# State updates of the running streams from operands already on chip: masked copies of B and 32-row products in place of two DRAM round trips

## The chip, the cores and the metric

The kernel runs on one core of one Trainium2 chip. The metric is device time in microseconds of one execution; the median of several is given. The engines are called by their short names in the profile: PE is the matrix engine (PEld its weight loads), DVE is VectorE, ACT is ScalarE, POOL is GpSimd, SP is the queue that issues most transfers. PSUM is the memory that PE writes its products to, in banks of 512 floats per partition; SBUF is the on-chip memory that everything else works in.

## The reference

One step of a layer with two parallel branches (causal pooling, and a Mamba-2 state-space branch, SSD) and an MLP, for 256 frames of a new stream and 16 frames each of 8 running streams, 384 rows in all. Model width 2048, 64 heads of 64 in 8 groups, state size 128, one layer, all in float32. The change concerns the last line of the scan, the new state of the running streams:

```python
def step(h, inp):
    xc, dtc, Bc, Cc = inp
    cum = jnp.cumsum(dtc * A, axis=1)
    ...
    xdt = xc * dtc[..., None]
    ...
    last = cum[:, -1]
    w_end = jnp.exp(last[:, None] - cum)
    h = h * jnp.exp(last)[..., None, None] + jnp.einsum('bsgn,bsgr,bsgrp->bgrpn', Bc, w_end, xdt)
    return h, y
```

For each of the 8 streams, group g and head, the new state is the decayed old one plus a sum over that stream's 16 frames of B (128 values a frame) times the weighted input (64 values a frame).

## The kernel before

Activations are held transposed (channels on partitions, 384 rows along the free axis). Every large product is done in three passes of a 32-bit matrix format: each operand is split into a high part h (a ScalarE copy that rounds) and a low part l (VectorE subtracts h from the original), and PE adds h·h, h·l and l·h. Weights come in slices of 128x1024 by an SP transfer (`wfetch`, line 63) and are split by lines 70 and 71 into three buffers each; `take` keeps up to three slices split ahead.

The state-space stage (lines 543 to 929) runs over eight groups g. In each, PE makes ten projections of two slices each: B, C, four blocks of x, four of the gate z (tiles `pj_x` and `pj_z`). The first six pass through a causal convolution (`conv_in`, `taps`, tiles cbuf, cacc, xs), which reads the old convolution state from `cstate`. Between projections stand short runs of small products, called lumps. A group has two pairs of channel blocks, jp = 0 and 1, and each pair S (four heads) has:

- `t_trx`: x is transposed to frames on partitions (`trx`, two PSUM banks); VectorE multiplies it by step-size weights into `xdt` and `xdw` (`xside`), and `xdw` is split into `xhl`, high and low (lines 729, 730);
- `t_trB`, once a group: B transposed the same way, split into `Bhl` (lines 685, 686);
- `t_cb` and `mside`: products of C and B, masked into `cbm`; `eside`: exponentials `E` on ScalarE;
- `t_yi`: the old states times C; `dside`: the old states `hs` are decayed; `t_Y`, `t_yT`: the outputs Y;
- `t_pp`: the new stream's state from `Bhl` and `xhl`;
- `state` (`t_su`, line 771 on): the running streams' update, eight products into four PSUM banks `su`, which VectorE adds to `hs` (line 786); then POOL's queue stores `hs`.

A lump is appended to PE's order with `lump`, so PE runs the lumps and projections in program order; on the other engines a scheduler orders the instructions at build time, by estimated times and by when tiles come free. Mid-group the order is pp, trx, cb, trB, yT, Y, yi and then su of the pair before; at the group's end it is pp, trx, yT, Y, yi, su.

In the block of the running streams, rows of `Bhl` and `xhl` are frames: stream b holds partitions 16b to 16b+15. A product that contracts over partitions can separate streams only if they lie on rows of their own, and PE's row strips begin at multiples of 32 or 64. The kernel before therefore stores the running streams' part of `Bhl` and `xhl` to DRAM (`b_scr`, `x_scr`, lines 688 and 733) and loads it back rearranged into `bst` and `xst` (lines 692 and 737): each stream gets 64 rows, four blocks of its 16 frames, with the four combinations of high and low parts of the two operands. One product over 64 rows then gives a stream's update with all its splits at once. Two streams stand on the two halves of the rows, and four positions along the free axis hold the eight streams.

All PSUM results outside the accumulating `mm` tiles (two banks) come from a pool of six banks, `sstile`. SBUF pools of a stage are stacked, so their tiles lie where tiles of the stage before were, and their first writes wait for those. `phd` holds most tiles of this stage and `phd1`, on top of it, the convolution state `cstate`, the buffers `cbuf` and, before the change, `bst`.

Of the kernel before, what the change touches and what calls it, by code (L numbers as in the profile page):

```python
# [6 lines left out]
F32 = mybir.dt.float32  # L7
F32R = mybir.dt.float32r
I32 = mybir.dt.int32
AF = mybir.ActivationFunctionType  # L10
ALU = mybir.AluOpType
# [3 lines left out]
P = 128  # L15
# [3 lines left out]
TS_ = 16  # L19
DM = 2048  # L20
KD = DM // P
G = 8
# [5 lines left out]

C_IDENT, C_ONES, C_MASK, C_CM, C_BM = 0, 128, 256, 768, 1024
C_RC, C_SCAN, C_END = 1032, 1096, 1504  # L30
V_GPRE, V_GMLP, V_PSC, V_CW, V_CB, V_NRM, V_DSK, V_DTB, V_ALOG, V_END = 0, 16, 32, 48, 240, 288, 320, 352, 353, 384


def build(ctx, tc, io):
    nc = tc.nc
    v, s, te, gp, sy = nc.vector, nc.scalar, nc.tensor, nc.gpsimd, nc.sync
# [5 lines left out]
    dram = ctx.enter_context(tc.tile_pool(name="dram", bufs=1, space=DRAM))  # L42
# [3 lines left out]
    vec = consts.tile([P, V_END], F32, name="vec")  # L46
# [6 lines left out]
    def sstile(name):  # L53
        return pss.tile([P, 512], F32, tag="ss", name=name)
# [27 lines left out]
    def woven(a):  # L82
        return a.rearrange("p (a n) -> p n a", a=2)

    def pairs(a):
        return a.rearrange("p (n a) -> p n a", a=2)
# [111 lines left out]
    a_scr = [dram.tile([P, T], F32, name=f"a_scr{i}") for i in range(32)]  # L198
    ma_scr = [dram.tile([P, T], F32, name=f"ma_scr{i}") for i in range(KD)]
    gb_scr = [dram.tile([P, T], F32, name=f"gb_scr{i}") for i in range(KD)]  # L200
    b_scr = [dram.tile([P, 2, P], F32, name=f"b_scr{i}") for i in range(G)]
    x_scr = [dram.tile([P, 2, 2, P], F32, name=f"x_scr{i}") for i in range(16)]
    cum_scr = dram.tile([NH, T], F32, name="cum_scr")
    dec_scr = dram.tile([NH, NB], F32, name="dec_scr")

# [149 lines left out]
    with tc.tile_pool(name="phc", bufs=1, reuse_waits="tile") as pc, tc.tile_pool(name="phc2", bufs=2, reuse_waits="tile") as pc2:  # L355
        pst = pc.tile([P, KD, NB, 15], F32, name="pst")
        gp.dma_start(pst, io["state_pool"])
        bufs = []
# [184 lines left out]
    with tc.tile_pool(name="phd", bufs=2, reuse_waits="tile") as pd, tc.tile_pool(  # L543
        name="phd1", bufs=1, reuse_waits="tile"
# [4 lines left out]
        for i in range(3):  # L549
            b = pd1.tile([P, 24, 19], F32, name=f"cbuf{i}")  # L550
            gp.memset(b[:, 0, :3], 0.0)
            cbuf.append(b)
        bst = []
        for i in range(2):
            bst.append(pd1.tile([P, 4, P], F32R, name=f"bst{i}"))
        seg = lambda a: a.rearrange("p (b t) -> p b t", b=24)
        ncv = [0]

# [33 lines left out]
        def lump(fn):  # L592
            with behind(last[0]):
                last[0] = fn()
# [87 lines left out]
        def bside(D):  # L682
            D.Bhl = pd.tile([P, 2, 3, P], F32R, tag="Bhl", name=f"Bhl{D.g}")
            bh, bl = (D.Bhl[:, a].rearrange("p b n -> p (b n)") for a in range(2))
            s.activation(bh, D.tr[:, :T], AF.Copy)
            v.tensor_tensor(bl, D.tr[:, :T], bh.bitcast(F32), ALU.subtract)
            bscr = b_scr[D.g]
            sy.dma_start(bscr, D.Bhl[:, :, 2, :].bitcast(F32))
            D.bs = bst[D.g % 2]
            for p4 in range(4):  # L690
                for h2 in range(2):
                    sy.dma_start(
                        D.bs[h2 * 64 + p4 * 16 : h2 * 64 + p4 * 16 + 16].bitcast(F32),
                        bscr.rearrange("(q h r) l n -> h l r q n", q=4, h=2)[h2, p4 // 2],
                    )

        def cside(D):
            D.Cm = pd.tile([P, 2, P], F32, tag="Cm", name=f"Cm{D.g}", bufs=1)
# [11 lines left out]
        def xside(S):  # L710
            S.xdt = pd.tile([P, 2, 3, P], F32, tag="xdt", name=f"xdt{S.nm}")
            S.xdw = pd.tile([P, 2, 3, P], F32, tag="xdw", name=f"xdw{S.nm}", bufs=1)
            for q, tv in enumerate(S.trs):
                for o, i in ((S.xdt, 3), (S.xdw, 6)):
                    v.tensor_tensor(
                        o[:, q].rearrange("p b (h q) -> p b h q", h=2),
                        tv,
                        tok[:, i : i + 3, S.h0 + q * 2 : S.h0 + q * 2 + 2].unsqueeze(3).to_broadcast([P, 3, 2, 64]),
                        ALU.mult,
                    )  # L720
            S.yis = pd.tile([P, 2, P], F32, tag="yis", name=f"yis{S.nm}", bufs=1)
            v.tensor_tensor(
                S.yis.rearrange("p j (h q) -> p (j h) q", h=2),
                S.yi.rearrange("p (h q) -> p h q", h=4),
                tok[:, 10, S.h0 : S.h0 + 4].unsqueeze(2).to_broadcast([P, 4, 64]),
                ALU.mult,
            )
            S.xhl = pd.tile([P, 2, 2, 3, P], F32R, tag="xhl", name=f"xhl{S.nm}", bufs=1)
            s.activation(S.xhl[:, 0], S.xdw, AF.Copy)
            v.tensor_tensor(S.xhl[:, 1], S.xdw, S.xhl[:, 0].bitcast(F32), ALU.subtract)  # L730
            xscr = x_scr[S.qd]
            for l in range(2):
                sy.dma_start(xscr[:, l], S.xhl[:, l, :, 2, :].bitcast(F32))
            S.xst = pd.tile([P, 4, 2 * P], F32R, tag="xst", name=f"xst{S.nm}", bufs=1)
            for p4 in range(4):
                for h2 in range(2):
                    sy.dma_start(
                        S.xst[h2 * 64 + p4 * 16 : h2 * 64 + p4 * 16 + 16].bitcast(F32),
                        xscr.rearrange("(q h r) l j n -> h l r q (j n)", q=4, h=2)[h2, p4 % 2],
                    )  # L740

        def eside(S, q):
            if q == 0:
# [24 lines left out]

        def state(S):
            def t_su():  # L770
                hs = S.hs.rearrange("p (r h) n -> p h r n", h=2)
                for r2 in (0, 2):
                    su = [sstile(f"su{S.nm}_{r2}_{h}") for h in range(2)]
                    for r in range(2):
                        for h in range(2):
                            t = slice(h * 64, h * 64 + 64)
                            i = te.matmul(
                                pairs(su[h][:, r * 256 : r * 256 + 256]),
                                S.D.bs[t, r2 + r, :],
                                woven(S.xst[t, r2 + r, :]),  # L780
                                start=True,
                                stop=True,
                            )
                    for h in range(2):
                        hr = hs[:, h, r2 : r2 + 2].rearrange("p r (a n) -> p r a n", a=2)
                        v.tensor_tensor(hr, hr, su[h].rearrange("p (r n a) -> p r a n", r=2, a=2), ALU.add)
                return i

            lump(t_su)
            gp.dma_start(io["new_ssm_s"][S.qd], S.hs)  # L790
# [52 lines left out]
        for g in range(G + 1):  # L843
# [17 lines left out]
            D = Pair()  # L861
# [17 lines left out]
            S = D.p[0]  # L879
# [4 lines left out]
            lump(lambda: t_cb(D))  # L884
            lump(lambda: t_trB(D))
            bside(D)
            if g:
                lump(lambda: t_yT(prev.p[1]))
                lump(lambda: t_Y(prev.p[1]))
            lump(lambda: t_yi(S))  # L890
            xside(S)
            mside(D)
            if g:
# [29 lines left out]
            lump(lambda: t_Y(S))  # L923
            lump(lambda: t_yi(S1))
            xside(S1)
            state(S)
            final(S)
# [6 lines left out]
    with ExitStack() as phe:  # L934
# [21 lines left out]
        for i in range(KD):  # L956
# [4 lines left out]
            h = mp.tile([P, T], F32R, name=f"mh{i}")  # L961
            l = mp.tile([P, T], F32R, name=f"ml{i}")
# [9 lines left out]
    r2 = res.tile([P, T], F32, name="r2")  # L972
# [32 lines left out]
    with tc.tile_pool(name="phf", bufs=1, side="right", reuse_waits="tile") as pf, tc.tile_pool(  # L1005
        name="phf2", bufs=2, side="right", reuse_waits="tile"
# [240 lines left out]
    with tc.tile_pool(name="phg", bufs=1, reuse_waits="tile") as pg, tc.tile_pool(  # L1247
        name="phg2", bufs=2, reuse_waits="tile"
# [8 lines left out]
        for c8 in range(NC):  # L1257
            hh = []
            for f8 in range(8):
                f = c8 * 8 + f8  # L1260
                ps = ups[f] if f < 3 else proj([io["w_up"][f, 0], io["w_up"][f, 1]], xs2, f"up{f}")
                t = pg2.tile([P, T], F32, tag="t", name=f"ht{f}")
# [5 lines left out]
                h = pg2.tile([P, T], F32R, tag=f"hh{f8}", name=f"hh{f}", bufs=1)  # L1268
                l = pg2.tile([P, T], F32R, tag=f"hl{f8}", name=f"hl{f}", bufs=1)
# [162 lines left out]
```

## Time and profile before

| | before |
|---|---|
| median of 3 runs | 2654.41 us (2653.67 to 2655.11) |
| the profiled execution, its own time | 2654.76 us |
| its span (first to last instruction) | 2653.0 us |
| mean granted PE clock | 0.999 |
| PE busy | 2640.3 us, 16181 products |
| DVE busy | 1528.4 us, 2152 instructions |
| ACT busy | 1171.7 us, 1828 instructions |
| state-space stage, from the first B projection to the last su | about 423 to 1175 us of the span |

A PE duration is from issue to the end of the write; products are pipelined, so the next one starts long before the end of the last, and the step from start to start is what a product costs. A row of a timeline reads: start in us, duration in us, engine, line, operation, output tile <- inputs, shape, count of like instructions merged into the row, and in brackets the engine's idle time before it and what ended that. A row of waits reads: who waited <- for whom: total us, times, the longest.

### The profile page before, as it was taken

To read this page: it belongs to the slowest core of one execution; us is meant where nothing else is said; L and a number is where in the kernel's file an instruction comes from. 1 tells how busy PE (TensorE), PEld (TensorE's weight loads), DVE (VectorE), ACT (ScalarE), POOL (GpSimd) and SP (SyncE) were. 2 spreads that over 40 slices of the span, in tenths; PEclk is the share of its full clock that TensorE was granted. 3 is DMA by queue.
4 is the path that set the end of the run, shared out by engine and by line. 5 is a ranking of instruction groups with operands and counts; after the bars stand their busy time and mean duration, and the time that the engine had idled before them with its cause. 6 is when DMAs were issued, how large, how long until landed. Compare 5 with 4: busy or idle time off the path is not lost.

```text
span 2653.0 us, 40481 instructions
## 1 busy us (share of the span) xinstructions
PE 2640.3 (100%) x16181; PEld 2539.1 (96%) x16181; DVE 1528.4 (58%) x2152; ACT 1171.7 (44%) x1828; POOL 150.5 (6%) x198
## 2 busy tenths in 40 slices
PE   9999999999999999999999999999999999999998
PEld 9999999999999999999999989999999999989897
DVE  6685334788788888767444436534444444444446
ACT  6443325557565756645333335433333333323233
POOL 0000000011111111020000000000000000000000
PEclk9999999999999999999999999999999999999999
DMA  7444445556666666667554553444444444444443
GB/s 274 146 135 154 147 147 203 194 203 218 207 227 208 211 226 214 224 208 246 177 161 160 186 162 132 143 135 135 135 135 135 135 136 135 136 134 136 136 137 131
DMA packets 147196, 451.48 MB, mean 170 GB/s; under 512 B 18432, under 2 KB 45632, under 8 KB 142016
## 3 DMA queue, kind: packets, MB, share of 16 engines
q1 hardware_dynamic: 134400, 389.90, 44.6%
q0 software_dynamic: 12608, 59.00, 5.9%
q8 instruction: 127, 2.08, 0.3%
q14 instruction: 61, 0.50, 0.1%
HBM read 407.11 MB, written 41.72 MB: 169 GB/s over the span
## 4 chain that ended last, share of the span: by engine, by line
PE 98%; DVE 1%; ACT 1%; issue 0%; DMA 0%; DVEq 0%; ACTq 0%
PE pj_up L98 6%; PE pj_up L99 6%; PE pj_up L100 6%; PE wd L145 6%; PE wd L143 6%; PE wd L144 6%; PE pj_x L98 5%; PE pj_x L100 4%; PE pj_x L99 4%; PE pj_sp L98 3%; PE pj_sp L100 3%; PE pj_z L100 3%; PE pj_z L99 3%; PE pj_sp L99 3%; PE pj_z L98 3%; PE pj_gb L98 2%
## 5 line engine op out<-in xcount | busy, mean ns | idle before, releaser
L98 PE MATMUL pj_up<-x1h,wh_up 128*128 128x384 f32 (+1 forms) x1024 | 333.7, 326 | 0.0
L99 PE MATMUL pj_up<-x1l,wh_up 128*128 128x384 f32 (+1 forms) x1024 | 333.4, 326 | 0.0
L100 PE MATMUL pj_up<-x1h,wl_up 128*128 128x384 f32 (+1 forms) x1024 | 333.4, 326 | 0.0
L71 DVE TENSOR_TENSOR wl_wd<-w_wd,wh_wd 128x1024 fp32r<-128x1024 f32 x126 | 154.4, 1225 | 240.0 <-ACT wh_wd L70 239.8
L143 PE MATMUL wd<-wh_wd,hh 128*128 128x512 f32 x756 | 286.5, 379 | 0.0
L144 PE MATMUL wd<-wl_wd,hh 128*128 128x512 f32 x756 | 286.5, 379 | 0.0
L145 PE MATMUL wd<-wh_wd,hl 128*128 128x512 f32 x756 | 286.5, 379 | 0.0
L70 ACT ACTIVATE wh_wd<-w_wd 128x1024 fp32r<-128x1024 f32 x126 | 133.3, 1058 | 321.6 <-PE wd L145 261.2
L70 ACT ACTIVATE wh_up<-w_up 128x1024 fp32r<-128x1024 f32 x126 | 133.3, 1058 | 292.5 <-PE pj_up L99 231.6
L71 DVE TENSOR_TENSOR wl_up<-w_up,wh_up 128x1024 fp32r<-128x1024 f32 x126 | 154.4, 1225 | 178.8 <-ACT wh_up L70 178.7
L98 PE MATMUL pj_x<-xgh,wh_x 128*128 128x384 f32 x768 | 252.0, 328 | 0.0
L100 PE MATMUL pj_x<-xgh,wl_x 128*128 128x384 f32 x768 | 250.6, 326 | 1.1 <-DVE wl_x L71 1.1
L99 PE MATMUL pj_x<-xgl,wh_x 128*128 128x384 f32 x768 | 250.4, 326 | 0.0
L99 PEld LDWEIGHTS pj_up<-x1l,wh_up 128*128 128x128 f32 x1024 | 193.6, 189 | 0.2
L98 PEld LDWEIGHTS pj_up<-x1h,wh_up 128*128 128x128 f32 x1024 | 193.6, 189 | 0.2
L100 PEld LDWEIGHTS pj_up<-x1h,wl_up 128*128 128x128 f32 x1024 | 193.6, 189 | 0.0
L98 PE MATMUL pj_z<-xgh,wh_z 128*128 128x384 f32 x512 | 166.9, 326 | 0.0
L99 PE MATMUL pj_z<-xgl,wh_z 128*128 128x384 f32 x512 | 166.9, 326 | 0.0
L100 PE MATMUL pj_z<-xgh,wl_z 128*128 128x384 f32 x512 | 166.9, 326 | 0.0
L98 PE MATMUL pj_sp<-abh,wh_sp 128*128 128x384 f32 x512 | 166.9, 326 | 0.0
L99 PE MATMUL pj_sp<-abl,wh_sp 128*128 128x384 f32 x512 | 166.9, 326 | 0.0
L100 PE MATMUL pj_sp<-abh,wl_sp 128*128 128x384 f32 x512 | 166.9, 326 | 0.0
(333 smaller groups left out, 6124.8 us busy)
## 6 DMA issues: line engine op xcount, KB each, us to landing
w_up<-w_up SPq DMA_DIRECT2D x128, 512.0 KB, 3.5
w_wd<-w_down SPq DMA_DIRECT2D x128, 512.0 KB, 3.5
w_x<-w_in SPq DMA_DIRECT2D x96, 512.0 KB, 3.6
w_z<-w_in SPq DMA_DIRECT2D x64, 512.0 KB, 3.6
w_sp<-w_ssd SPq DMA_DIRECT2D x64, 512.0 KB, 3.5
w_ga<-w_ga SPq DMA_DIRECT2D x32, 512.0 KB, 3.5
w_pp<-w_pp SPq DMA_DIRECT2D x32, 512.0 KB, 3.5
hs<-ssm POOLq DMA_DIRECT2D x16, 1024.0 KB, 6.3
```

What stands on the lines that cost most here:

```text
L70: cut[0] = s.activation(h, w, AF.Copy)
L71: cut[1] = v.tensor_tensor(l, w, h.bitcast(F32), ALU.subtract)
L98: te.matmul(out, wh, xh, start=first, stop=False, **how)
L99: te.matmul(out, wh, xl, start=False, stop=False, **how)
L100: return te.matmul(out, wl, xh, start=False, stop=last, **how)
L143: te.matmul(out, mh, vh, start=k == 0, stop=False)
L144: te.matmul(out, mh, vl, start=False, stop=False)
L145: last[0] = te.matmul(out, ml, vh, start=False, stop=k == nk - 1)
```

## The change

The round trips through DRAM go. B of the running streams is copied twice on ScalarE with a per-partition factor of 0 or 1: copy h keeps the streams of parity h and holds zeros for the others. Every quarter of 32 rows holds two streams, one of either parity, so a product over a quarter of rows with copy h gives the update of one stream alone. The product is taken straight from `xhl`, where it lies. The three split combinations are now three accumulating products instead of blocks of rows: 2 parities x 3 combinations x 4 quarters, 24 products of 32 rows a pair, into four PSUM banks, one for each quarter, where there were 8 products of 64 rows. VectorE still makes four additions a pair.

```diff
-V_GPRE, ..., V_ALOG, V_END = 0, 16, 32, 48, 240, 288, 320, 352, 353, 384
+V_GPRE, ..., V_ALOG, V_PAR, V_END = 0, 16, 32, 48, 240, 288, 320, 352, 353, 354, 384
...
-    b_scr = [dram.tile([P, 2, P], F32, name=f"b_scr{i}") for i in range(G)]
-    x_scr = [dram.tile([P, 2, 2, P], F32, name=f"x_scr{i}") for i in range(16)]
...
-        bst = []
-        for i in range(2):
-            bst.append(pd1.tile([P, 4, P], F32R, name=f"bst{i}"))
...
             v.tensor_tensor(bl, D.tr[:, :T], bh.bitcast(F32), ALU.subtract)
-            bscr = b_scr[D.g]
-            sy.dma_start(bscr, D.Bhl[:, :, 2, :].bitcast(F32))
-            D.bs = bst[D.g % 2]
-            for p4 in range(4):
-                for h2 in range(2):
-                    sy.dma_start(
-                        D.bs[h2 * 64 + p4 * 16 : h2 * 64 + p4 * 16 + 16].bitcast(F32),
-                        bscr.rearrange("(q h r) l n -> h l r q n", q=4, h=2)[h2, p4 // 2],
-                    )
+            D.Bm = pd.tile([P, 2, 2, P], F32R, tag="Bm", name=f"Bm{D.g}", bufs=1)
+            for h in range(2):
+                s.activation(
+                    D.Bm[:, h],
+                    D.Bhl[:, :, 2, :].bitcast(F32),
+                    AF.Copy,
+                    scale=vec[:, V_PAR + h : V_PAR + h + 1],
+                )
...
             v.tensor_tensor(S.xhl[:, 1], S.xdw, S.xhl[:, 0].bitcast(F32), ALU.subtract)
-            xscr = x_scr[S.qd]
-            for l in range(2):
-                sy.dma_start(xscr[:, l], S.xhl[:, l, :, 2, :].bitcast(F32))
-            S.xst = pd.tile([P, 4, 2 * P], F32R, tag="xst", name=f"xst{S.nm}", bufs=1)
-            for p4 in range(4):
-                for h2 in range(2):
-                    sy.dma_start(
-                        S.xst[h2 * 64 + p4 * 16 : h2 * 64 + p4 * 16 + 16].bitcast(F32),
-                        xscr.rearrange("(q h r) l j n -> h l r q (j n)", q=4, h=2)[h2, p4 % 2],
-                    )
...
             def t_su():
-                hs = S.hs.rearrange("p (r h) n -> p h r n", h=2)
-                for r2 in (0, 2):
-                    su = [sstile(f"su{S.nm}_{r2}_{h}") for h in range(2)]
-                    for r in range(2):
-                        for h in range(2):
-                            t = slice(h * 64, h * 64 + 64)
+                su = [sstile(f"su{S.nm}_{q}") for q in range(4)]
+                for h in range(2):
+                    for n, (bl, xl) in enumerate(((0, 0), (0, 1), (1, 0))):
+                        for q in range(4):
+                            t = slice(q * 32, q * 32 + 32)
                             i = te.matmul(
-                                pairs(su[h][:, r * 256 : r * 256 + 256]),
-                                S.D.bs[t, r2 + r, :],
-                                woven(S.xst[t, r2 + r, :]),
-                                start=True,
-                                stop=True,
+                                pairs(su[q][:, h * 256 : h * 256 + 256]),
+                                S.D.Bm[t, h, bl, :],
+                                S.xhl[t, xl, :, 2, :].rearrange("p j n -> p n j"),
+                                start=n == 0,
+                                stop=n == 2,
                             )
-                    for h in range(2):
-                        hr = hs[:, h, r2 : r2 + 2].rearrange("p r (a n) -> p r a n", a=2)
-                        v.tensor_tensor(hr, hr, su[h].rearrange("p (r n a) -> p r a n", r=2, a=2), ALU.add)
+                for q in range(4):
+                    hr = S.hs[:, 2 * q : 2 * q + 2].rearrange("p h (a n) -> p h a n", a=2)
+                    v.tensor_tensor(hr, hr, su[q].rearrange("p (h n a) -> p h a n", h=2, a=2), ALU.add)
                 return i
...
+    for h in range(2):
+        vec[:, V_PAR + h] = (np.arange(P) // TS_) % 2 == h
```

More of the change, by code (lines that the diff above doesn't have):

```diff
@@ L30 @@
 C_RC, C_SCAN, C_END = 1032, 1096, 1504
-V_GPRE, V_GMLP, V_PSC, V_CW, V_CB, V_NRM, V_DSK, V_DTB, V_ALOG, V_END = 0, 16, 32, 48, 240, 288, 320, 352, 353, 384
+V_GPRE, V_GMLP, V_PSC, V_CW, V_CB, V_NRM, V_DSK, V_DTB, V_ALOG, V_PAR, V_END = 0, 16, 32, 48, 240, 288, 320, 352, 353, 354, 384
 def build(ctx, tc, io):
```

## The prediction

> **What bounds the kernel now.** I read the page first: busy shares, then the chain that ended last.
>
> ```profile
> PE 2640.3 (100%) x16181; PEld 2539.1 (96%) x16181; DVE 1528.4 (58%) x2152; ACT 1171.7 (44%) x1828; POOL 150.5 (6%) x198
> PE 98%; DVE 1%; ACT 1%; issue 0%; DMA 0%; DVEq 0%; ACTq 0%
> ```
>
> The matrix engine is the chain: 98% of the end time is its own instructions, and no share is put down to DMA. The next question is how much of its time is waiting, which the view of waits for that engine answers in full:
>
> ```profile
> PE pj_ga L100 <- DVE wl_ga L71: 1.5, 1, 1.5
> PE warm_o L231 <- DVE warm L227: 1.2, 1, 1.2
> PE pj_x L100 <- DVE wl_x L71: 1.1, 2, 0.9
> PE pj_p L307 <- ACT xgh L267: 0.3, 1, 0.3
> ```
>
> That is 4.1 us in the whole run, and only the 1.1 us at pj_x lies in the state-space stage that the change touches. So work taken off the DMA queues can give the matrix engine at most 1.1 us there; whatever is added to the matrix engine's own stream is paid in full. The third view is the timeline of that engine at the end of a group, where a pair's state update (su) stands between yi and the next projection:
>
> ```profile
> 504.21 0.83 PE L672 MATMUL py<-xhl,Bhl 128*128 128x256 f32 x6
> 505.84 1.95 PE L658 MATMUL Y<-E,xdt 128*32 128x256 f32 x48
> 507.60 1.08 PE L637 MATMUL py<-hs,Cm 128*32 128x256 f32 x16
> 508.61 0.71 PE L777 MATMUL su<-xst,bst 64*128 64x256 f32 x8
> 509.26 0.43 PE L98 MATMUL pj_x<-xgh,wh_x 128*128 128x384 f32 x1
> ```
>
> and the view of the su tiles for all pairs:
>
> ```profile
> L777 PEld LDWEIGHTS su<-xst,bst x128: 182/187/188, 508.6 to 1172.6; 64*128 64x128 f32 x128
> L777 PE MATMUL su<-xst,bst x128: 272/272/373, 508.6 to 1172.7; 64*128 64x256 f32 x128
> L786 DVE TENSOR_TENSOR hs<-hs,su x64: 680/687/692, 509.8 to 1175.2; 128x512 f32<-128x512 f32 x64
> ```
>
> A product's duration is mostly latency; what counts is the step from start to start. In py (full height, 256 columns, the shape that su also moves) six products span 0.83 us and one lasts 0.275, so the step is (0.83 - 0.275)/5 = 0.111 us. In su eight products span 0.71 us and the last lasts 0.272, so the last starts 0.44 us after the first. The first is stretched to 0.373, 0.10 over the median, while it waits for its weights; that leaves 0.34 us for three steps, 0.113 us each. So eight half-height products are four rounds of two, and the two of a round run side by side. A narrower window of the same timeline shows such a round, and a round of four in Y, the only place with four products at once:
>
> ```profile
> 508.61 0.38 PE L777 MATMUL su<-xst,bst 64*128 64x256 f32 x2
> 505.84 0.42 PE L658 MATMUL Y<-E,xdt 128*32 128x256 f32 x4
> L658 PE MATMUL Y<-E,xdt 128*32 128x256 f32 x256 | 20.1, 385 | 0.0
> ```
>
> **The product term.** The change makes 24 products of 32 rows out of 8 of 64, in the order h, n, q: the four quarters q follow each other, so they can be rounds of four, six rounds where there were four. If four quarters overlap as two halves do, a pair costs two more rounds, 2 x 0.113 = 0.226 us, and two more staggered starts in a round, some 0.006 us (two products of 0.373 take 0.38): 0.232 us. Nothing stands beside it: the chain runs through these products. 16 pairs x 0.232 = 3.7 us. The nearest row that shows four at once is Y's: four products on four column strips are over in 0.42 us where one takes 0.385. So loads and products of four strips overlap, and the engine can start four within some 0.04 us, a third of a round. No row shows four row strips, nor four accumulators written at once. The bound above is that only two overlap: twelve rounds, eight more than now, 8 x 0.113 = 0.90 us a pair, 14.5 us. The bound below is two rounds at the py step with nothing for the stagger, 2 x 0.111 x 16 = 3.6 us. I take 3.7: halves of rows and strips of columns both overlap fully here, so the lower end is far the nearer.
>
> The Trainium skill's "TensorE: Matmul & The Clock Gate", section Part 3 on packing small matmuls, speaks to this in two ways. Its span rule (one duration plus about 4 ns per further tile) gives the 3.7 us above. Its table gives 3.07 times for four 32-row tiles of 512 columns, not four times; an estimate by that ratio is a round of 4 x 0.111/3.07 = 0.145 us, a pair 6 x 0.145 - 4 x 0.113 = 0.42 us longer, and 6.7 us for the term. No run here shows a 32-row product, so that stays open and enters below as a rival.
>
> **What leaves the DMA queue.** These issues go from the SP queue:
>
> ```profile
> L737 SPq DMA_DIRECT2D xst<-x_scr x128: 302/425/1844, 472.3 to 1145.9; - x128
> L733 SPq DMA_DIRECT2D x_scr<-xhl x32: 372/378/1215, 467.0 to 1140.2; - x32
> L692 SPq DMA_DIRECT2D bst<-b_scr x64: 325/426/1351, 468.7 to 1098.1; - x64
> L688 SPq DMA_DIRECT2D b_scr<-Bhl x8: 518/519/580, 466.3 to 1091.6; - x8
> ACT wh_x L70 <- PE pj_z L99: 53.0, 20, 2.8
> SPq L63 <- DVE wl_x L71: 251.5, 86, 7.4
> ```
>
> 232 issues at some 0.4 us are about 98 us of that queue, and w_x and w_z fetches queue behind them. The last two rows say why this gives nothing: the weight split waits for the matrix engine to give a buffer back, not for its data, and the fetch waits for the split. Both stay as they are. I book 0.
>
> **What is added off the chain.** ScalarE gets two copies of 128x256 for each of eight groups. The nearest rows, with the xhl copy beside them:
>
> ```profile
> L757 ACT ACTIVATE E<-E 128x256 f32<-128x256 f32 x32 | 13.1, 409 | 0.1
> L795 ACT COPY pe<-py 128x256 f32<-128x256 f32 x15 | 5.5, 363 | 4.3 <-DVE yis L722 4.3
> L729 ACT ACTIVATE xhl<-xdw 128x768 fp32r<-128x768 f32 x16 | 13.5, 846 | 13.1 <-DVE xdw L715 13.1
> ```
>
> so 0.36 to 0.41 us each, 0.8 us a group. They wait for the low half of B on VectorE and, as Bm has one buffer, for the su of the group before, mid-group; they are wanted at the group's end, some 45 us on (from one su to the next, 508.61 to 553.97 below). VectorE keeps four adds of 0.687 a pair; they start behind all six rounds instead of two, 4 x 0.113 = 0.45 us later, and behind them waits the store of hs on POOL's queue, whose buffer comes back a half group later. Booked at 0.
>
> There is one new wait. The products now read xhl itself, which has one buffer, so the next pair's xhl copy (0.85 us on ScalarE, 0.96 on VectorE behind it) must wait for su to end, where it used to run at or before it. Behind it on ScalarE stand the exponentials E and the next weight splits. The tightest split in the steady groups is this one:
>
> ```profile
> 564.46 1.05 ACT L70 ACTIVATE wh_z<-w_z 128x1024 fp32r<-128x1024 f32 x1
> 567.30 1.21 DVE L71 TENSOR_TENSOR wl_z<-w_z,wh_z 128x1024 fp32r<-128x1024 f32 x1
> 570.64 0.33 PE L100 MATMUL pj_z<-xgh,wl_z 128*128 128x384 f32 x1
> 553.08 0.85 ACT L729 ACTIVATE xhl<-xdw 128x768 fp32r<-128x768 f32 x1 [1.50 <-DVE xdw L715]
> 553.08:567.00 13.92, 13.92 (x104) 13.29 (x98) 13.92 (x18) 13.84 (x28) 4.63 (x5) 1.00 0.55 186
> L586 ACT ACT_TABLE_LOAD x24 | 30.8, 1283 | 0.4
> ```
>
> Counting splits and products in order, eight wl products to a split, this wl_z is the one that the product at 570.64 uses first: ready at 568.51, 2.13 us of cover. The fifth row gives busy times for PE, PEld, VectorE, ScalarE, POOL from 553.08 to 567: VectorE and ScalarE have no gap there, so added work does push the splits. But the two Bm copies (0.8) fit into the cover, with 0.85 of moved xhl as well, and the 1.50 us that ScalarE idles ahead of xhl can now go to E. I book 0.
>
> The four accumulators are also wanted at once, instead of two and two. What frees the last of them, at the group's end and mid-group:
>
> ```profile
> 507.92 0.55 DVE L715 TENSOR_TENSOR xdw<-trx,tok 128x384 f32<-128x384 f32 x1
> 552.96 0.69 DVE L708 TENSOR_TENSOR cbm<-cb,cst 128x512 f32<-128x512 f32 x1
> 553.97 0.71 PE L777 MATMUL su<-xst,bst 64*128 64x256 f32 x8
> ```
>
> 508.47 against a start at 508.61, and 553.65 against 553.97: 0.14 and 0.32 us of cover, enough if VectorE keeps its order. If one 0.55 us operation slips ahead, 0.41 us at eight pairs is 3.3 us.
>
> **A by-effect in SBUF.** xst (4 KB a partition) goes and Bm (2 KB) comes in the first pool of the stage, so its second pool, which begins with cstate, moves 2 KB down. There the stage loses time today:
>
> ```profile
> 424.86 0.54 POOL L547 DMA_DIRECT2D cstate<-state_conv  x1 [1.87 <-DMA ma_scr<-sg]
> 432.78 0.22 ACT L572 COPY cbuf<-cstate 128x24 f32<-128x24 f32 x1 [2.67 <-DMA cstate<-state_conv]
> ```
>
> cstate's load waits 1.87 us for the last store from an sg tile, and ScalarE then stands 2.67 us with weight splits behind; the 1.1 us of pj_x waits follow in the same group. Adding up tile sizes, cstate overlaps the first sg buffer by under 1 KB, so 2 KB lower it is clear of it. Bounds: 0 if the order in that group is otherwise tight, -1.1 if all of it goes; I take -1.1, as 1.87 exceeds the sum.
>
> **Sum.** 3.7 - 1.1 = +2.6 us. The profiled execution took 2654.76 us (span 2653.0), the median is 2654.41; on the median that is 2657.0. Its own bounds are +2.5 to +4.8 (no by-effect and a stall of 1.1): 2656.9 to 2659.2. That is 0.1%, under the 0.2% (5.3 us) that a measurement of this kernel can tell from no change.
>
> **Rivals.** (1) Four quarters overlap only in part. For: no row shows it, and the accumulators written at once double. Against: every packed row here overlaps fully. Price between 3.7 and 14.5 us; halfway 9.1, less 1.1: +8.0, 2662.4; at the end 2667.8. Chance 0.13. By the ratio in the skill's table alone it would be 2660.0.
>
> (2) The other side: the split at 570.64 comes late, from ScalarE. The copies (0.8), the moved xhl (0.85) and one more table load (1.28 where they occur) make 2.93 against 2.13 of cover, 0.80 us in each of seven groups, 5.6 us; with 2.6 that is 2662.6. It decides when that wl_z ends after 570.64. For: both helpers are full from 553 to 567. Against: the 1.50 us before xhl, and a table load comes only if the order changes. The accumulator slip (3.3 us) would add here. Chance 0.18.
>
> (3) The change gains. The matrix engine's rows hold 1.1 us of waits and the cost of switching the tile shape: from su's last start (509.05) to pj_x at 509.26 is 0.21 us for a step of 0.113, and pj_x lasts 0.43 for 0.33, together 0.2 us, and as much ahead of su. If half of that went, 16 x 0.2 = 3.2 us, the sum would be -0.6 us: 2653.8. Beyond 5.3 us there is no row to pay it. Chance 0.06, half of it beyond.
>
> **Numbers.** Forecast 0.63. Within 0.2%: 0.63 and half of rival 3, 0.66. Slower: rivals 1 and 2, 0.31. Faster: 0.03. The range runs from 2655.0 to 2664.0: it takes in the forecast and the nearer parts of rivals 1 and 2, and leaves out the two-at-a-time end, a pile of both stalls, and a real gain, under 2 in 10.
>
> **What the changed profile would show.** Right: 384 su products of 32x256 in 16 bursts of about 0.94 us, starts in fours, rounds of 0.113; the projection follows 0.88 us after su's first start (0.65 now); no PE wait on wl_z or on VectorE before su; cstate's load without the sg wait; SP short of 232 issues with ring waits grown instead. Wrong: rounds of 0.14 or more (rival 1); a PE wait of some tenths in every group (rival 2); bursts as short as now.

## The result and the profile after

The median after is 2667.68 us (2667.25 to 2669.39, 4 runs) against 2654.58 us before (2653.67 to 2655.11, 4 runs): a ratio of 1.0051, 95% interval 1.0034 to 1.0068. The change costs 13.1 us. The prediction said 2657.0 and a range to 2664.0, so it missed by 10.7 us and the range did not hold. The profiled execution took 2668.06 us, its span 2666.3, at the same granted clock, 0.999.

From the page after, the busy shares and the shares of the chain that ended last:

```profile
PE 2646.8 (99%) x16437; PEld 2542.6 (95%) x16437; DVE 1524.0 (57%) x2152; ACT 1157.9 (43%) x1830; POOL 139.2 (5%) x198
PE 93%; ACT 3%; DVE 3%; POOL 1%; issue 0%; DMA 0%; DVEq 0%; ACTq 0%
```

DVE, ACT and POOL are each less busy than before. Yet 7% of the chain now lies off the matrix engine, where it was 2%, and POOL is among those that hold it. The view of waits for PE after says where (who waited <- for whom: total us, times, longest):

```profile
PE pj_z L100 <- DVE wl_z L71: 5.4, 6, 0.9
PE pj_z L98 <- ACT wh_z L70: 2.8, 6, 0.5
```

Both rows are new, six times each; the pj_x row of before is gone. The timeline of PE in the second group shows one such pair of stalls:

```profile
568.95 0.33 PE L100 MATMUL pj_z<-xgh,wl_z 128*128 128x384 f32 x1
569.75 0.43 PE L98 MATMUL pj_z<-xgh,wh_z 128*128 128x384 f32 x1 [0.47 <-ACT wh_z L70]
570.01 0.33 PE L99 MATMUL pj_z<-xgl,wh_z 128*128 128x384 f32 x1
571.24 0.43 PE L100 MATMUL pj_z<-xgh,wl_z 128*128 128x384 f32 x1 [0.90 <-DVE wl_z L71]
571.51 0.33 PE L98 MATMUL pj_z<-xgh,wh_z 128*128 128x384 f32 x1
```

The undisturbed step is 0.1625 us. From 568.95 to 569.75 is 0.64 more than one step, from 569.75 to 571.51 it is 1.27 more than three. That is 1.91 us a group, of which the view of waits counts only 1.37: a product's row lasts two steps, so part of each gap looks busy. Measured so, from start to start, the six groups lose 11.5 us.

The products themselves, in the timeline of PE and the view of the su tiles after:

```profile
506.95 0.94 PE L760 MATMUL su<-xhl,Bm 32*128 32x256 f32 x24
507.82 0.43 PE L98 MATMUL pj_x<-xgh,wh_x 128*128 128x384 f32 x1
L760 PE MATMUL su<-xhl,Bm x384: 270/270/372, 506.9 to 1186.2; 32*128 32x256 f32 x192
```

The stage from the first pj_x to the last pj_z, by the views of these tiles, before and then after:

```profile
L98 PE MATMUL pj_x<-xgh,wh_x x768: 326/326/430, 421.2 to 1101.1; 128*128 128x384 f32 x192
L100 PE MATMUL pj_z<-xgh,wl_z x512: 326/326/326, 473.3 to 1132.9; 128*128 128x384 f32 x171
```

```profile
L98 PE MATMUL pj_x<-xgh,wh_x x768: 326/326/430, 421.2 to 1112.2; 128*128 128x384 f32 x192
L100 PE MATMUL pj_z<-xgh,wl_z x512: 326/326/430, 471.7 to 1145.9; 128*128 128x384 f32 x171
```

It grew from 711.7 to 724.7 us, 13.0 (12.9 unrounded), which is nearly the whole difference; the last two of the 16 bursts of su stand behind it. Read from start to start, three terms make it up:

| term | working | us |
|---|---|---|
| su bursts | 14 in this stretch, each 0.228 longer | +3.2 |
| first group, projections held by cstate | 1.97 lost before, 0.22 after | -1.75 |
| z projections, six of seven groups | 1.91 each | +11.5 |
| sum | | +12.9 |

The first two are the prediction's own terms. The third is the miss. Its origin, in the timelines of ScalarE, POOL and VectorE after, in that group:

```profile
554.19 0.52 ACT L797 ACTIVATE ysq<-zs 128x384 f32<-128x384 f32 x1
554.84 3.27 POOL L798 TENSOR_TENSOR ssum<-ssum,ysq 128x384 f32<-128x384 f32 x1
554.96 2.29 DVE L746 TENSOR_TENSOR hs<-hs,decb 128x2048 f32<-128x2048 f32 x1
558.15 0.52 ACT L797 ACTIVATE ysq<-zs 128x384 f32<-128x384 f32 x1 [2.87 <-POOL ssum L798]
558.58 0.89 ACT L684 ACTIVATE Bm<-Bhl,vec 128x256 fp32r<-128x256 f32 x2
559.38 0.82 ACT L723 ACTIVATE xhl<-xdw 128x768 fp32r<-128x768 f32 x1
568.65 1.04 ACT L70 ACTIVATE wh_z<-w_z 128x1024 fp32r<-128x1024 f32 x1
569.97 1.22 DVE L71 TENSOR_TENSOR wl_z<-w_z,wh_z 128x1024 fp32r<-128x1024 f32 x1
```

`ysq` holds the square of an output, has one buffer, and POOL adds it to `ssum`. The second square must wait for the first sum to give the buffer back. In the kernel before, xhl and most exponentials stood ahead of both squares, and a weight split and further exponentials between them, so that wait was covered:

```profile
558.98 0.52 ACT L814 ACTIVATE ysq<-zs 128x384 f32<-128x384 f32 x1
559.40 1.05 ACT L70 ACTIVATE wh_z<-w_z 128x1024 fp32r<-128x1024 f32 x1
559.58 1.04 POOL L815 TENSOR_TENSOR ssum<-ssum,ysq 128x384 f32<-128x384 f32 x1 [0.99 <-ACT ysq L814]
562.10 0.52 ACT L814 ACTIVATE ysq<-zs 128x384 f32<-128x384 f32 x1
```

After, ScalarE's queue, which was ordered at build time, has both squares ahead of xhl and of most exponentials, with two exponentials between them. It stands 2.87 us, with Bm, xhl, the other exponentials and the splits of w_z behind it. The sum lasts 3.27 us instead of 1.04; it now falls together with VectorE's decay of `hs`, and e7 below tests whether that is why. The chain of waits between 550 and 572 us goes just that way, from one sum to the late product (Bm, xhl, exponentials and a split stand between the square and wl_z):

```profile
554.84 3.28 POOL ssum L798
...
558.15 0.52 ACT ysq L797
...
569.97 1.23 DVE wl_z L71
...
571.24 0.43 PE pj_z L100
```

One group is an experiment that the kernel makes by itself. Near 1016 us the same two instructions meet at the same distance, and the other one pays:

```profile
1015.89 1.06 POOL L798 TENSOR_TENSOR ssum<-ssum,ysq 128x384 f32<-128x384 f32 x1
1016.01 3.09 DVE L746 TENSOR_TENSOR hs<-hs,decb 128x2048 f32<-128x2048 f32 x1
1016.98 0.52 ACT L797 ACTIVATE ysq<-zs 128x384 f32<-128x384 f32 x1 [0.65 <-POOL ssum L798]
```

The sum takes 1.06 us there, ysq waits 0.65, and this is the one group of the seven without a z stall.

### The profile page after: what moved, and what is told of

It reads as the page before. It is cut to its first block, busy times and chain, and to the rows that moved or that the text cites. A ratio compares the mean times of both kernels' runs of the same rounds, so it can differ in the third digit from the quotient of the medians.

```text
span 2666.3 us, 40656 instructions
## 1 busy us (share of the span) xinstructions
PE 2646.8 (99%) x16437; PEld 2542.6 (95%) x16437; DVE 1524.0 (57%) x2152; ACT 1157.9 (43%) x1830; POOL 139.2 (5%) x198
## 4 chain that ended last, share of the span: by engine, by line
PE 93%; ACT 3%; DVE 3%; POOL 1%; issue 0%; DMA 0%; DVEq 0%; ACTq 0%
PE pj_up L100 6%; PE pj_up L98 6%; PE pj_up L99 6%; PE wd L145 6%; PE wd L143 6%; PE wd L144 6%; PE pj_x L98 4%; PE pj_x L99 4%; PE pj_x L100 4%; PE pj_sp L100 3%; PE pj_sp L99 3%; PE pj_sp L98 3%; PE pj_z L100 3%; PE pj_z L98 2%; PE pj_z L99 2%; PE pj_gb L98 2%
```

## The experiments

Theory A: the stall is ysq's wait, and that wait came because xhl, which may now not start before su has ended, was put behind the squares at build time. The rivals: the two Bm copies fill ScalarE (Theory B, part of the prediction's second rival), the transfers of w_z come late (Theory C), or the new wait of xhl for su itself. The last is not in the trace: in the kernel after, none of ScalarE's idle time ahead of its 16 xhl copies is ended by su, so its one buffer acts through the order alone. The medians, and the stage length from the first pj_x to the last pj_z:

| kernel | median us | ratio to before, 95% | stage us |
|---|---|---|---|
| before | 2654.4 to 2654.6 | | 711.7 |
| after | 2667.68 | 1.0051 (1.0034 to 1.0068) | 724.7 |
| e1_ysq2 | 2657.79 | 1.0013 (1.0004 to 1.0021) | 714.5 |
| e2_xhl2 | 2657.75 | 1.0012 (1.0003 to 1.0021) | 714.7 |
| e3_bm_once | 2670.02 | 1.0059 (1.0045 to 1.0072) | 726.9 |
| e4_before_down | 2653.64 | 0.9998 (0.9989 to 1.0007) | 709.8 |
| e5_ysq2_down | 2656.17 | 1.0006 (0.9998 to 1.0015) | 713.6 |
| e6_one_combo | 2673.35 | 1.0076 (1.0061 to 1.0092) | 727.2 |
| e7_decay_late | 2664.49 | 1.0037 (1.0023 to 1.0051) | 715.7 |

**e1_ysq2: after, with a second buffer for ysq.**

```diff
-                    qs = pd.tile([P, T], F32, tag="ysq", name=f"ysq{g}_{j}", bufs=1)
+                    qs = pd.tile([P, T], F32, tag="ysq", name=f"ysq{g}_{j}", bufs=2)
```

> The changed kernel with two buffers for ysq instead of one; ScalarE's order round it stays, but for the two ysq now standing together. Theory A (ScalarE stands 2.87 us in its queue at the second ysq, which waits for GpSimd's sum to give the one buffer back; the split of the second z projection comes late by 1.9 us in six of seven groups, 11.5 us in all): the wait and the 11.5 us go, 2656.2 us. Theory B (the two Bm copies alone, 0.8 us a group, are the cost): little changes, 2667 us, with PE still waiting at pj_z. Theory C (the transfers of w_z come late, behind the loads of cbc): 2667 us, with ScalarE waiting for w_z instead.

2657.79 us: 9.9 us of the 13.1 are gone. The timelines of ScalarE and POOL in the same group, where rows of one kind are merged:

```profile
555.36 0.95 ACT L797 ACTIVATE ysq<-zs 128x384 f32<-128x384 f32 x2
556.02 4.95 POOL L798 TENSOR_TENSOR ssum<-ssum,ysq 128x384 f32<-128x384 f32 x2
556.79 0.89 ACT L684 ACTIVATE Bm<-Bhl,vec 128x256 fp32r<-128x256 f32 x2
```

Squares and Bm (xhl behind them) keep the order of after, and POOL needs 4.95 us for its two sums beside the decay, but ScalarE no longer stands still at the second square, and PE waits for no z split. So the order alone does not hurt; the wait inside it does. Late transfers are not the cause either: in the kernel after, ScalarE starts each of the late splits of w_z without idle time, and in e5, where no z projection stalls, it waits longer for w_z in all (21.9 us against 17.1). The 1.5 KB of the new buffer push cstate up again, and this row of PE's waits is back:

```profile
PE pj_x L100 <- DVE wl_x L71: 0.9, 1, 0.9
```

The first group loses 1.56 us by its starts, where after lost 0.22; that is most of the 1.6 us above theory A's number.

**e2_xhl2: after, with a second buffer for xhl,** so that no copy waits for su.

```diff
-            S.xhl = pd.tile([P, 2, 2, 3, P], F32R, tag="xhl", name=f"xhl{S.nm}", bufs=1)
+            S.xhl = pd.tile([P, 2, 2, 3, P], F32R, tag="xhl", name=f"xhl{S.nm}", bufs=2)
```

> The changed kernel with two buffers for xhl, so the next pair's copy needn't wait for su; ScalarE's order is then that of the kernel before (xhl ahead of the exponentials, the two ysq apart), with Bm in between. If the one buffer of xhl is the root of the changed order and with it of theory A: about 2656 us, and no wait of ysq for GpSimd; the tightest split keeps some 1.3 us (2.13 less 0.8 for Bm). Theory B: a stall stays, 2661 to 2667 us.

2657.75 us, the same gain from the other end. ScalarE, POOL and VectorE in the group:

```profile
553.47 0.84 ACT L723 ACTIVATE xhl<-xdw 128x768 fp32r<-128x768 f32 x1 [1.50 <-DVE xdw L709]
556.48 0.52 ACT L797 ACTIVATE ysq<-zs 128x384 f32<-128x384 f32 x1
557.43 1.02 POOL L798 TENSOR_TENSOR ssum<-ssum,ysq 128x384 f32<-128x384 f32 x1
560.87 0.51 ACT L797 ACTIVATE ysq<-zs 128x384 f32<-128x384 f32 x1
563.01 2.28 DVE L746 TENSOR_TENSOR hs<-hs,decb 128x2048 f32<-128x2048 f32 x1
```

The order of before is back: xhl first, the squares 4.4 us apart, the first sum 1.02 us, and the decay only at 563.01, with both sums over. ysq is left with its one buffer, the Bm copies with their two per group, and no z projection stalls. So the root is that xhl's single buffer is now read by su. As in e1, the new buffer (6 KB) pushes cstate up, and the first group loses 1.69 us by its starts, which is most of the 1.8 us above the expected 2656.

**e3_bm_once: after, with the Bm copies made in the first group only.**

```diff
-            D.Bm = pd.tile([P, 2, 2, P], F32R, tag="Bm", name=f"Bm{D.g}", bufs=1)
-            for h in range(2):
-                s.activation(
+            if D.g == 0:
+                D.Bm = pd.tile([P, 2, 2, P], F32R, tag="Bm", name=f"Bm{D.g}", bufs=1)
+                for h in range(2):
+                    s.activation(
...
+                Bm0[0] = D.Bm
+            D.Bm = Bm0[0]
```

> The changed kernel with the Bm copies made for the first group only; later groups' states are computed from the first group's B, so that part of the result is left out. ScalarE's order stays as in the changed kernel without Bm. Theory A: the 2.87 us wait of ysq stays, 0.8 us of queue behind it goes, so the stall of 1.9 us shrinks to about 1.1 us in six groups: 2663 us. Theory B: all of the 11.5 us goes, 2656 us. Theory C: 2667 us.

2670.02 us: no faster than after. The copies as cause are refuted: the stall stays without them, 1.8 to 2.0 us in all seven groups, and e2 has the copies without the stall. ScalarE there:

```profile
557.21 0.52 ACT L802 ACTIVATE ysq<-zs 128x384 f32<-128x384 f32 x1 [2.86 <-POOL ssum L803]
564.19 0.51 ACT L186 ACTIVATE nh_g<-ssum 128x384 fp32r<-128x384 f32 x1
567.43 1.04 ACT L70 ACTIVATE wh_z<-w_z 128x1024 fp32r<-128x1024 f32 x1
569.39 1.05 ACT L70 ACTIVATE wh_z<-w_z 128x1024 fp32r<-128x1024 f32 x1
```

Theory A's number for it missed too. It took the 0.8 us of the copies off the path, but the build reordered again: nh_g, which after ran at 569.60 behind the split at 568.65, now stands ahead of both. Time freed on a full queue did not reach the step that was late.

**e7_decay_late: after, with the first pair's decay given a later place.**

```diff
-            dside(S)
+            with later():
+                dside(S)
```

> The changed kernel with VectorE's decay of the pair's states (128x2048, 2.29 us) forced behind the latest weight split, out of the way of GpSimd's sum; ysq keeps its one buffer, and ScalarE's order is the same through both ysq, Bm and xhl. If GpSimd's sum takes 3.27 us because VectorE's decay holds the port to SBUF that the two share: the sum is down to 1.0 to 1.6 us, ScalarE's wait at the second ysq to 0.6 to 1.2 us from 2.87, and the stall in the z projections shrinks to nothing or a few tenths, 2656 to 2659 us. If the sum is long for another reason: still 3.3 us, 2667 us.

POOL and ScalarE in the group:

```profile
555.21 1.06 POOL L798 TENSOR_TENSOR ssum<-ssum,ysq 128x384 f32<-128x384 f32 x1
556.30 0.53 ACT L797 ACTIVATE ysq<-zs 128x384 f32<-128x384 f32 x1 [0.65 <-POOL ssum L798]
```

Without the decay beside it the sum is back to 1.06 us, ysq waits 0.65, and the z stall is gone with one buffer each for ysq and xhl. So the decay is what makes the sum slow. The time itself missed the expected 2656 to 2659: 2664.49 us, with runs from 2659.95 to 2668.14, where the profile is that of the fastest run (span 2658.2). In it the su burst at the group's end, 0.87 us from its first load to the next projection's in the kernel after, takes 1.12 to 1.52 us in seven groups, 3.0 us more in all. PE has a new row of waits that covers a part of it:

```profile
597.61 1.36 PE L760 MATMUL su<-xhl,Bm 32*128 32x256 f32 x24
PE su L760 <- DVE xdw L709: 0.5, 2, 0.3
```

The row of su above stands where VectorE is still reading one of the four PSUM banks that su wants, until 597.92 us. Why the other runs are up to 8 us longer stays open.

**e4_before_down: before, with two small tiles moved into the second pool,** so that cstate lies 2 KB lower, as the change puts it.

```diff
-            S.yis = pd.tile([P, 2, P], F32, tag="yis", name=f"yis{S.nm}", bufs=1)
+            S.yis = pd1.tile([P, 2, P], F32, tag="yis", name=f"yis{S.nm}", bufs=1)
...
-            pe = pd.tile([P, 2, P], F32, tag="pe", name=f"pe{S.nm}", bufs=1)
+            pe = pd1.tile([P, 2, P], F32, tag="pe", name=f"pe{S.nm}", bufs=1)
```

> The kernel before with two small tiles (yis and pe, 2 KB a partition) moved from the stage's first pool to the end of its second, so that cstate lies 2 KB lower, as in the changed kernel; every engine's order stays. If the place of cstate is what freed the first group: its load no longer waits for the store from sg, ScalarE gets it some 1.8 us earlier, the three short waits of PE in the first group go: 2654.6 - 1.8 = 2652.8 us. If the gain there came from the queue or the order: 2654.6 us.

The stage is 709.8 us, 1.9 shorter. POOL and ScalarE in the first group:

```profile
423.88 0.54 POOL L547 DMA_DIRECT2D cstate<-state_conv  x1
425.56 0.20 POOL L551 MEMSET cbuf<- 128x3 f32 x3 [1.13 <-DMA ma_scr<-sg]
431.75 0.20 ACT L572 COPY cbuf<-cstate 128x24 f32<-128x24 f32 x1
```

The load goes out without a wait (1.87 us before), ScalarE no longer stands at cbuf (2.67 before), and PE has no pj_x wait. The median, 2653.64 us, is the lowest of all kernels here, but the ratio's interval holds 1.

**e5_ysq2_down: after, with e1's and e4's edits together.**

> The changed kernel with two ysq buffers and with yis and pe moved to the second pool, so that cstate lies low again. If the changed kernel's time is a plain sum (products +3.65 us from 16 bursts of 0.87 for 0.64 us, cstate's place -1.75 us, ysq's wait +11.5 us), this one has the products and the gain alone: stage longer than that of the low kernel before by 3.65 us, and 1.5 us less than with two ysq buffers alone: 2656 to 2657.3 us, PE's waits in the stage under 0.3 us. If the two ysq buffers only hid something else: 2658 us or more, with waits of PE in other places.

2656.17 us, as expected, with 1 inside the interval. Between e4 and e5 lies the change without its two side effects: 713.6 - 709.8 = 3.8 us of stage, by starts 14 bursts of 0.228 and 0.56 lost in the first group. (The medians differ by 2.5 us. In e5's profile the stage begins 1.9 us earlier; the stages ahead of it have the same code and vary by that much.)

**e6_one_combo: e5, with only the high-by-high products,** 8 instead of 24 a pair.

```diff
-                    for n, (bl, xl) in enumerate(((0, 0), (0, 1), (1, 0))):
+                    for n, (bl, xl) in enumerate(((0, 0),)):
...
-                                stop=n == 2,
+                                stop=True,
```

> The kernel with two ysq buffers and low cstate, with one of the three split combinations in the state products (high part by high part), so 8 products in two rounds of four in place of 24 in six; the two small corrections of the states are left out. If rounds of four stand on the chain at 0.112 us each: bursts of 0.42 us, 16 x 4 x 0.112 = 7.1 us less, about 2649.5 us. If a burst is hidden or set by something else than its rounds: less than 3 us of gain.

As a price of a round it worked; as a time it missed by 24 us. PE's timeline and its waits:

```profile
506.87 0.49 PE L760 MATMUL su<-xhl,Bm 32*128 32x256 f32 x8
PE bc_g L190 <- ACT nh_g L186: 9.0, 7, 1.3
```

The burst shrinks from 0.94 to 0.49 us, 0.45 for four rounds, 0.112 each. But a shorter su gave the build another order again, and PE now waits for the group norm's split (nh_g, and nl_g behind it) in seven groups, 2.89 us each from start to start, 20 us. That accounts for the profiled run, the fastest at 2669.79 us; the others go up to 2677.22. What makes nh_g late stays open. One lead, not tested: ScalarE loads a function table five times between 561 and 575 us there (ACT_TABLE_LOAD, 1.28 us each), where e5 does so once.

## Why the prediction was wrong

**What bounds the kernel: right, but it proved too little.** PE's own stream is paid in full, as said. But a view with 4.1 us of waits shows where there is no slack today, not what slack is left after the queues are ordered anew.

**The product term: right.** 0.232 us a pair was booked; the time from su's first load to the next projection's grew by 0.228 in all 16 (0.870 from 0.642), 3.65 us. Products start in fours within 10 ns, the first round takes 213 ns, the later ones 110 to 113. Four row quarters and four banks overlap fully, so rival 1 is out. The span rule of the Trainium skill's "TensorE: Matmul & The Clock Gate", Part 3, agrees with these rows. Its table's 3.07 times would, by the prediction's estimate, be rounds of 0.145 us; no row here shows that, and the measurement decides.

**The by-effect in SBUF: right in cause, too small.** -1.1 us was booked from the waits, which count idle time only; the starts give -1.75, and e4 shows it by itself at -1.9. The two booked terms together came to +1.9 us for the +2.6 of the forecast, so the miss lies outside them.

**The DMA queue: right.** 232 issues went, and PE gained nothing from it: the one wait that left its list in this stage, at pj_x, went with cstate's place, as e4 shows.

**The step that failed** is "There is one new wait", where xhl's wait for su was booked at nothing. It was costed in the order of before: ScalarE's 1.50 us of idle time ahead of xhl would take the exponentials, and the cover of 2.13 us at the z split would hold 0.8 and 0.85 of moved work. But the queue is ordered at build time, and with a later xhl the two squares moved ahead of it. There the covered wait for POOL became an open one of 2.87 us, more than the cover. Rival 2 named the right place and victim (a z split late from ScalarE, in about seven groups, by work that moves), with 0.80 us a group for 1.91, and from the wrong work: e3 takes the copies away and the stall stays; e1 takes ysq's wait away and it goes; e2 takes the reason for the new order away and it goes too. The extra table load of rival 2 did not come: ScalarE makes 41 in the kernel after, 55 before. Of the range: 11.5 us is twice the 5.6 of rival 2, and no bound of it was worked out for a queue that stands still.

**The accumulators: right here.** PE waits for nothing before su in the kernel after. In e7, where VectorE's order changed, the wait for xdw that the prediction described did appear: by the starts 0.25 to 0.65 us at seven pairs, 3.0 us in all, for the 0.41 at eight pairs, 3.3 us, that it had priced.

## What to carry to other kernels

When a change makes a single-buffered tile live longer, the cost to look for isn't its own wait, but what the scheduler puts in front: list what may overtake it on its queue, and which of those wait for a slow engine. Here either of two second buffers (ysq or xhl) gave back 9.9 us. And an experiment that shortens a step rebuilds every queue: e3 and e6 both missed, with queues in another order than expected, so the order of the rows must be compared before a difference in time is read.

## What the runs showed of the hardware

POOL's sum of 128x384 and VectorE's product of 128x2048, both float32 from and to SBUF, hold each other up: beside each other one takes its usual time and the other waits. The sum takes 3.27 us with a decay of 2.29, or 1.06 with a decay of 3.09; apart they take 1.00 to 1.07 and 2.28. The sum's loss, 2.2 us, is about the whole of the decay, and the decay's loss, 0.8, most of the sum. In the two cases the sum's row starts 0.12 us ahead of the decay's, so the start in the trace does not say which will wait. Not every operation of VectorE does this: beside the additions of line 769, which take one of their two inputs from PSUM, the sum takes 1.02 us (e2). The Trainium skill's "SBUF — State Buffer", section "SBUF: two separate sides", describes such a pair of ports, shared by VectorE and GpSimd and held for a whole instruction by the one that starts first. The sizes agree with it; that the first one wins is not what these rows show by their starts.
